# Token-major projections of two slots at a time with 512 moving columns, and one doubling of the memory keys

## The chip, the core and the metric

The kernel runs on one core of one Trainium2 chip. The metric is the device time of one launch in microseconds (us). TensorE (PE) multiplies and transposes, VectorE (DVE), ScalarE (ACT) and GpSimd (POOL) do the element-wise work, and the DMA transfers of this kernel are issued from the queue of SyncE (SP) and, for a few tables, from POOL's.

## What is computed

One layer of an encoder trunk for one batch of 2048 tokens of width 1024. All mixers read one normed input through one projection of 11 slots of 256 columns:

```python
h = rmsnorm(x, norm_g[l])
proj = h @ w_in[l]
a_u, a_v, a_g, b_q, b_k, b_v, b_g, c_in, c_g, d_q, d_g = jnp.split(proj, N_IN_SLOTS, axis=-1)
y_a = chunked_spatial_gating(a_u, a_v, ...) * jax.nn.silu(a_g)
y_b = neighbourhood_attention(b_q, b_k, b_v, ...) * jax.nn.silu(b_g)
y_c = fourier_mixing(c_in, fn_w[l]) * jax.nn.silu(c_g)
mem_n = rmsnorm(mem, mem_norm_g[l])
y_d = memory_attention(d_q, mem_n, w_mkv, ...) * jax.nn.silu(d_g)
x = x + jnp.concatenate([y_a, y_b, y_c, y_d], axis=-1) @ w_out[l]
```

The neighbourhood attention has 4 heads of 64 on a token grid of 32 rows by 64 columns, the memory attention 4 heads over 256 memory tokens; queries and keys of both are normed by head.

## The kernel before

Everything is float32. Each large product is made from a high and a low part of both operands (three matmuls: high by high, high by low, low by high). The tokens are worked in two halves `h` of 1024.

**The projection slots.** `slot` (L201) runs one slot of 256 columns for one half of the tokens into four PSUM banks `acc` (pool `ps_acc`, four banks in all). In the slots of `NATURAL` (L948: a_v, b_q, b_k, b_v, d_q) the tokens are the stationary side and the result has tokens on the partitions: 8 blocks of 128 tokens, two to a bank, 192 matmuls with 256 moving columns. The other slots have the weights on the stationary side and 512 tokens as moving columns, 96 matmuls a slot. One weight tile, 256 rows of `w_in` in 256 columns, serves 48 matmuls of a natural slot.

**The weights.** `get_w` (L187) loads a tile into `raw` (256 KB, SP queue), ACT casts the high part (L196) and POOL subtracts it for the low part (L198). The pool `wp` has six buffers "hilo", so three tiles of a high and a low part each can be there: one in use and two ahead, in every slot.

**What follows a slot.** The PSUM banks are read by ACT and DVE in turns (`evac_nat`, L307, into `nat`, five buffers). The queries and keys are normed (`head_norm`: POOL squares L323, DVE sums L325, POOL power through L108 and L109, DVE multiplies L328), transposed on PE, split, and written to DRAM. `do_bv` (L378) writes the values of the neighbourhood attention in parts of 256 columns (ACT L385, DVE L386). `do_a` (L583) norms a_v. `mem_kv` (L392) makes keys and values of the memory (matmuls into two `sc` banks, squares of the memory rows on ACT L420, then ACT L427 and L430 out of `sc`, head_norm), and `mem_k` (L438) doubles the columns of the keys with eight DVE copies of 128x128 (L447, two buffers `sq`), each before one transpose, in two groups of four.

**The order.** PE's order is fixed by hand. `drive` runs a generator of projection slots, then `out_proj`, and between its steps the tasks that were spawned with a delay: mixers, transposes, attention units. The delay counts in a planner's time, which adds up matmul columns. A task waits for names in `self.done`. The other engines' instructions are ordered by a scheduler with the priorities given by `hp`, and each engine runs its own row in that order. `main` (L978) has the order of slots; the neighbourhood attention is spawned at L1040 and starts when "fft", "b_q1" and "d_q1" are done. It opens its SBUF pool where the Fourier mixer's was, and loads `kk`, `kl`, `qq` (L784, L785), `vt` (L761) and `bt` (L771).

Of the kernel before, what the change touches and what calls it, by code (L numbers as in the profile page):

```python
# [20 lines left out]
GW = 256  # L21
HD = 64
# [25 lines left out]
class Kern:  # L48
# [151 lines left out]

    def slot(self, h, c0, natural, ps, kstep):  # L201
# [105 lines left out]
    def evac_nat(self, h, ps, bank):  # L307
        nc = self.nc
        q = self.nat.tile([128, 512], F32, name="nat")
        with self.hp(8000):  # L310
            for j in range(2):
                o, i = q[:, j * 256:(j + 1) * 256], ps[bank][:, j * 256:(j + 1) * 256]
                r = self.rstd[h][:, bank * 2 + j:bank * 2 + j + 1]
                if j:
# [16 lines left out]
    def transpose_pairs(self, q):  # L331
        ps = self.ps_mi.tile([128, 512], F32, name="mi")
        for pr in range(2):
            for j in range(2):
                self.tr(ps[:, pr * 256 + j * 128:pr * 256 + j * 128 + 128],
                        q[:, j * 256 + pr * 128:j * 256 + pr * 128 + 128])
        return ps.rearrange("p (a b) -> p a b", a=2)

    def do_bqk(self, h, ps, kind, key):
        nc = self.nc  # L340
        with self.hp(8000):
            qs = [self.head_norm(self.evac_nat(h, ps, b)) for b in range(4)]
        yield 14.0 if key == "d_q0" else 6.5
        for b in range(4):
            with self.hp(8000):
                t = self.transpose_pairs(qs[b])
                hl = [self.st.tile([128, 2, 256], F32R, name="st") for _ in range(2)]
                hi, lo = hl
                for a in range(2):
                    ta, ha, la = t[:, a], hi[:, a], lo[:, a]  # L350
                    if kind == "q":
                        ta = ta.rearrange("p (r b c) -> p r b c", b=4, c=16)
                        ha, la = (v.rearrange("p (b r c) -> p r b c", b=4, c=16) for v in (ha, la))
                    elif kind == "k":
                        ta = ta.rearrange("p (r c) -> p r c", r=4)
                        ha, la = (v.rearrange("p (c r) -> p r c", r=4) for v in (ha, la))
                    if kind == "k":
                        nc.scalar.activation(out=ha, in_=ta, func=AF.Copy, scale=self.gqk[:, 0:1])
                        nc.vector.scalar_tensor_tensor(out=la, in0=ta, scalar=self.gqk[:, 0:1], in1=ha.bitcast(F32),
                                                       op0=ALU.mult, op1=ALU.subtract)  # L360
                    elif kind == "q":
                        self.evac_split(ha, la, ta)
                if kind == "d":
                    self.evac_split(hi, lo, t)
                gg = h * 4 + b
                for i in range(2):
                    src = hl[i].bitcast(F32)
                    if kind == "q":
                        nc.sync.dma_start(
                            out=self.QB[:, i, gg // 2, :, :, gg % 2, :].rearrange("p a b x -> p (a b) x"),  # L370
                            in_=src.rearrange("p a b -> p (a b)").rearrange("p (y x) -> p y x", x=64))
                    else:
                        dst = self.KB[i] if kind == "k" else self.QD[i]
                        nc.sync.dma_start(out=dst[:, :, gg * 256:(gg + 1) * 256], in_=src)
# [782 lines left out]
```

## Time and profile before

| | us |
|---|---|
| median of 3 runs (885.18 to 885.97) | 885.59 |
| profiled execution | 883.6 |
| its span, first to last instruction | 881.8 |
| PE busy | 860.3 (98% of the span) |
| DVE busy | 496.3 (56%) |
| ACT busy | 380.2 (43%) |
| POOL busy | 323.6 (37%) |

The page gives for each engine the time in which it worked. A wait of an engine is put down to the instruction that released it. For PE the page and the list of waits matter most: a stretch in which PE has no idle time has a length that is the number of its matmuls times the time from one start to the next, which I call the pitch. The granted clock of TensorE was 0.992 of full speed on average.

### The profile page before, as it was taken

The page shows a single profiled execution, that of the slowest core. Times are in us where ns is not written, and L with a number is a line of the kernel's source. Part 1 is how long each engine was busy: PE and PEld are TensorE (multiplying, and loading weights), DVE is VectorE, ACT ScalarE, POOL GpSimd, SP SyncE. Part 2 cuts the span into 40 slices and gives each one's busy share as a digit, 9 for nine tenths or more (in the row PEclk, how much of TensorE's full clock was granted, in tenths as well). Part 3 has the DMA queues.
Part 4 walks back from the last instruction along what each step waited for, and adds up shares of the span by engine and source line. Part 5 has one row for each costly group of instructions (what it writes and reads, how often), then busy time and mean ns, then how long its engine had stood idle before and what let it go on. Part 6 is the DMA issues. An engine that isn't in the chain of part 4 may idle for free. (4 is left out here: it accounts for less than half of the span.)

```text
span 881.8 us, 15020 instructions
## 1 busy us (share of the span) xinstructions
PE 860.3 (98%) x5216; PEld 757.5 (86%) x5216; DVE 496.3 (56%) x1084; ACT 380.2 (43%) x881; POOL 323.6 (37%) x354
## 2 busy tenths in 40 slices
PE   7999899999999999999999999999979999999998
PEld 6999689999878889999998788888868888888886
DVE  4336753776122746753246766676877776863331
ACT  5664333545532532332313445565874444531110
POOL 1148411752142222754165323453564433321110
PEclk8999999999999999999999999999999999999999
DMA  7956232336933661449669687865789977645752
GB/s 234 356 190 214 95 128 77 102 108 177 287 108 102 211 198 37 129 128 234 192 197 317 198 272 221 270 204 171 220 237 297 322 234 227 200 134 174 225 184 81
DMA packets 142717, 169.59 MB, mean 192 GB/s; under 512 B 28704, under 2 KB 104368, under 8 KB 142640
## 3 DMA queue, kind: packets, MB, share of 16 engines
q1 hardware_dynamic: 140912, 162.33, 58.6%
q0 software_dynamic: 1728, 6.29, 2.5%
q8 instruction: 41, 0.67, 0.3%
q14 instruction: 36, 0.29, 0.1%
HBM read 124.53 MB, written 44.05 MB: 191 GB/s over the span
## 5 line engine op out<-in xcount | busy, mean ns | idle before, releaser
L131 PE MATMUL acc<-hilo 128*128 128x512 f32 (+1 forms) x3648 | 716.2, 344 | 8.3 <-DVE st L296 4.9
L131 PEld LDWEIGHTS acc<-hilo 128*128 128x128 f32 x3648 | 560.3, 190 | 70.7 <-DVE st L296 5.7
L198 POOL TENSOR_TENSOR hilo<-raw,hilo 128x512 fp32r<-128x512 f32 x84 | 113.1, 1346 | 287.9 <-ACT hilo L196 268.4
L196 ACT CAST hilo<-raw 128x512 fp32r<-128x512 f32 x84 | 51.9, 618 | 109.9 <-PE acc L131 90.8
L904 POOL TENSOR_TENSOR nat<-nat 128x256 f32<-128x256 f32 x39 | 30.9, 794 | 111.2 <-DMA nat<-O 73.9
L458 DVE TENSOR_TENSOR PT<-mi,PT 128x512 fp32r<-128x512 f32 (+2 forms) x96 | 61.1, 637 | 9.5 <-ACT PT L457 9.5
L457 ACT CAST PT<-mi 128x512 fp32r<-128x512 f32 (+2 forms) x96 | 52.2, 544 | 26.9 <-PE mi L135 26.4
L910 ACT CAST hilo<-nat 128x256 fp32r<-128x256 f32 x64 | 26.0, 406 | 75.4 <-PE acc L131 65.0
L839 ACT ACTIVATE P<-P,smx 128x288 f32<-128x288 f32 (+1 forms) x64 | 39.8, 622 | 40.9 <-DVE smx L837 40.7
L135 PE MATMUL mi<-ident,P 128*128 128x128 f32 (+1 forms) x352 | 54.3, 273 | 2.4 <-DVE P L842 1.7
L135 PEld LDWEIGHTS mi<-ident,P 128*128 128x128 f32 (+1 forms) x352 | 42.4, 135 | 15.5 <-DVE PT L458 2.3
L296 DVE TENSOR_TENSOR st<-acc,rbc 128x512 f32<-128x512 f32 x32 | 21.9, 685 | 37.9 <-PE acc L131 36.1
L109 POOL TENSOR_TENSOR hss<-hss,mhalf 128x8 f32<-128x8 f32 x25 | 41.9, 1680 | 0.9
L879 POOL TENSOR_TENSOR ob<-tmp 64x128 f32<-64x128 f32 x64 | 29.5, 479 | 33.3 <-DVE tmp L875 30.3
L911 DVE TENSOR_TENSOR hilo<-nat,hilo 128x256 fp32r<-128x256 f32 x64 | 33.1, 526 | 14.7 <-ACT hilo L910 14.5
L530 ACT ACTIVATE P<-sc,smx 128x256 f32<-128x256 f32 x64 | 29.7, 469 | 22.6 <-DVE smx L526 22.5
L122 DVE SCALAR_TENSOR_TENSOR hilo<-raw,gcol,hilo 128x512 fp32r<-128x512 f32 x32 | 24.9, 796 | 22.5 <-ACT hilo L121 22.0
L842 DVE TENSOR_SCALAR P<-P,smx 128x288 f32<-128x288 f32 (+1 forms) x64 | 36.1, 564 | 1.8
L837 DVE CUSTOM_DVE_ANT_0 P<-sc,bt 128x288 f32<-128x288 f32 (+1 forms) x64 | 35.6, 556 | 2.1 <-DMA bt<-in_bias 0.9
L131 PEld LDWEIGHTS mi<-PT,vt 96*128 96x128 f32 (+1 forms) x160 | 28.3, 193 | 6.9 <-issue 0.7
L875 DVE TENSOR_TENSOR tmp<-mi,tmp 64x512 f32<-64x512 f32 x32 | 22.0, 687 | 20.4 <-ACT tmp L874 20.2
L131 PE MATMUL mi<-PT,vt 96*128 96x256 f32 (+3 forms) x160 | 32.5, 334 | 0.3 <-DVE PT L458 0.2
(152 smaller groups left out, 971.1 us busy)
## 6 DMA issues: line engine op xcount, KB each, us to landing
raw<-in_w_in SPq DMA_DIRECT2D x88, 256.0 KB, 3.5
raw<-in_xT SPq DMA_DIRECT2D x32, 256.0 KB, 3.5
nat<-in_x SPq DMA_DIRECT2D x32, 256.0 KB, 5.1
G<-st SPq DMA_DIRECT2D x32, 256.0 KB, 2.5
nat<-G SPq DMA_DIRECT2D x64, 128.0 KB, 2.4
st<-in_x SPq DMA_DIRECT2D x32, 256.0 KB, 4.7
out_y<-st SPq DMA_DIRECT2D x32, 256.0 KB, 3.8
tab<-in_dft_s POOLq DMA_DIRECT2D x12, 512.0 KB, 4.8
```

What stands on the lines that cost most here:

```text
L109: nc.gpsimd.tensor_tensor(out=out, in0=out, in1=self.mhalf[:, :n], op=ALU.pow)
L131: self.nc.tensor.matmul(out=out, lhsT=lhsT, rhs=rhs, start=start, stop=stop, **k)
L135: self.nc.tensor.transpose(out=out, in_=in_, identity=self.ident)
L196: nc.scalar.copy(out=w[0], in_=raw)
L198: eng.tensor_tensor(out=w[1], in0=raw, in1=w[0].bitcast(F32), op=ALU.subtract)
L457: self.nc.scalar.copy(out=hi, in_=src)
L458: (eng or self.nc.vector).tensor_tensor(out=lo, in0=src, in1=hi.bitcast(F32), op=ALU.subtract)
L837: nc.vector.tensor_tensor_reduce(out=P[:, :n], in0=sc[:, :n], in1=bt[:, :n], op0=ALU.add, op1=ALU.min, scale=-1.0, scalar=3e38, accum_out= ...
L839: nc.scalar.activation(out=P[:, :n], in_=P[:, :n], func=AF.Exp, bias=sm[:, 1:2], scale=-1.0, accum_out=sm[:, 2:3])
L842: nc.vector.tensor_scalar(out=P[:, :n], in0=P[:, :n], scalar1=sm[:, 3:4], scalar2=None, op0=ALU.mult)
L904: mul.tensor_tensor(out=g, in0=o, in1=g, op=ALU.mult)
L911: nc.vector.tensor_tensor(out=y[:, 1], in0=g, in1=y[:, 0].bitcast(F32), op=ALU.subtract)
```

## The change

`pair` runs two slots together: b_q with b_k (`pair_qk`) and a_v with b_v (`pair_vv`). For each half `u` of the 1024 tokens (512 tokens) it takes four blocks of 128 tokens, one PSUM bank each, with 512 moving columns: 256 of the one slot and 256 of the other. In each half of each pair there are 96 matmuls. With two pairs, two token halves `h` and two halves `u` that is 768 matmuls of 512 columns in the place of 1536 of 256. d_q stays as it was.

`get_w2` loads 128 rows of `w_in` in 2 x 256 columns, as one tile of the old size. Each step of `pair` (24 matmuls) uses two tiles, A and B: for each of the four token blocks three matmuls on A and then three on B. Each half `u` loads all eight tiles again: 64 tiles in the place of 32, so 32 more loads of 256 KB, 32 more casts on ACT and 32 more subtractions on POOL. The pool `wp` keeps its six buffers.

What follows a slot now runs per half `u`. In the pair of a_v and b_v the evacuation of a_v (`do_a`) is spawned and that of b_v (`do_bv`) runs at once, so it stands ahead; both read every bank of the half. In `mem_kv` one DVE operation doubles all 512 columns into a tile "PT", and the delay of `mem_k` is 8.0 for 7.0. The constants of a_v's mixer are a task with a wait of 12.0. The values pair comes first for the first 1024 tokens. The attention waits for "fft" and "b_qk1" alone.

```diff
+    def get_w2(self, k, ia, ib):
+        nc = self.nc
+        with self.hp(8000):
+            raw = self.raw.tile([128, 2, 256], F32, name="raw")
+            src = self.ins["w_in"][k * 128:(k + 1) * 128, :].rearrange("p (s c) -> p s c", c=GW)
+            nc.sync.dma_start(out=raw, in_=src[:, ia:ib + 1:ib - ia, :])
+            w = [self.wp.tile([128, 2, 256], F32R, name="hilo") for _ in range(2)]
+            nc.scalar.copy(out=w[0], in_=raw)
+            nc.gpsimd.tensor_tensor(out=w[1], in0=raw, in1=w[0].bitcast(F32), op=ALU.subtract)
+        return [v.rearrange("p a b -> p (a b)") for v in w]
+
+    def pair(self, h, ca, cb, fn):
+        for u in range(2):
+            ps = [self.ps_acc.tile([128, 512], F32, name="acc") for _ in range(4)]
+            for k0 in range(0, 8, 2):
+                ops = [(self.get_x(h, k)[u], self.get_w2(k, ca // GW, cb // GW)) for k in (k0, k0 + 1)]
+                for t in range(4):
+                    sl = slice(t * 128, (t + 1) * 128)
+                    for k, ((xh, xl), (wh, wl)) in enumerate(ops, k0):
+                        self.mm(ps[t], xh[:, sl], wh, k == 0, False)
+                        self.mm(ps[t], xh[:, sl], wl, False, False)
+                        self.mm(ps[t], xl[:, sl], wh, False, k == 7)
+                    yield
+            fn(h, u, ps)
...
-    def do_bv(self, h, ps):
-        nc = self.nc
+    def do_bv(self, h, u, ps):
+        nc = self.nc
         with self.hp(8000):
-            for t in range(8):
+            for j in range(4):
+                t = u * 4 + j
                 v = self.nat.tile([128, 4, 2, 64], F32R, name="nat")
-                p = ps[t // 2][:, (t % 2) * 256:(t % 2) * 256 + 256].rearrange("p (g d) -> p g d", d=HD)
+                p = ps[j][:, 256:512].rearrange("p (g d) -> p g d", d=HD)
...
-        self.spawn(self.mem_k(q), 7.0)
+        twice = self.att.tile([128, 512, 2], F32, name="PT", bufs=2)
+        nc.vector.tensor_copy(out=twice, in_=q.unsqueeze(2).broadcast_to([128, 512, 2]))
+        self.spawn(self.mem_k(twice), 8.0)
...
-                    twice = self.sqp.tile([128, HD, 2], F32, name="sq")
-                    nc.vector.tensor_copy(out=twice, in_=q[:, c0:c0 + HD].unsqueeze(2).broadcast_to([128, HD, 2]))
-                    self.tr(ps[:, hh, j * 128:j * 128 + 128], twice.rearrange("p d o -> p (d o)"))
+                    self.tr(ps[:, hh, j * 128:j * 128 + 128],
+                            twice[:, c0:c0 + HD].rearrange("p d o -> p (d o)"))
...
-    def do_a(self, h, ps):
+    def do_a(self, h, u, ps):
...
-            for b in range(4):
-                v = self.evac_nat(h, ps, b)
+            for b in range(2):
+                v = self.evac_nat(h, [(ps[2 * b + j][:, 0:256], u * 4 + 2 * b + j) for j in range(2)])
...
+    def pair_qk(self, h):
+        yield from self.pair(h, B_Q, B_K, lambda h, u, ps: self.spawn(self.do_bqk(h, u, ps), 0, -1))
+
+    def pair_vv(self, h):
+        def fn(h, u, ps):
+            self.spawn(self.do_a(h, u, ps), 0, -1)
+            self.do_bv(h, u, ps)
+        yield from self.pair(h, A_V, B_V, fn)
...
-        yield from self.proj(0, "a_v")
+        self.spawn(self.constants_a(), 0, -2)
+        yield from self.pair_vv(0)
         self.spawn(self.when(("mem", "d_q0"), lambda: self.pipeline(self.d_items(0, range(4)), DLY["d0"])), 0, 1)
-        self.constants_a()
         yield from self.proj(0, "a_u")
-        for q in ("b_k", "b_q", "b_v", "a_g"):
-            yield from self.proj(0, q)
+        yield from self.pair_qk(0)
+        yield from self.proj(0, "a_g")
...
-        yield from self.proj(1, "b_k")
-        yield from self.proj(1, "b_q")
-        yield from self.proj(1, "b_v")
+        yield from self.pair_qk(1)
+        yield from self.pair_vv(1)
...
-        self.spawn(self.when(("fft", "b_q1", "d_q1"), attn), 0, 1)
-        for q in ("d_q", "a_v", "a_u", "a_g", "d_g", "b_g", "c_g"):
+        self.spawn(self.when(("fft", "b_qk1"), attn), 0, 1)
+        for q in ("d_q", "a_u", "a_g", "d_g", "b_g", "c_g"):
             yield from self.proj(1, q)
```

**The first place: PE, where the Fourier mixer ends and the attention begins.** `sc<-tab,ab` are the mixer's last matmuls, `acc<-hilo` those of the running slot (d_q of the second half of the tokens), `kk`, `kl` and `qq` the attention's keys and queries. Before:

```order
L131 MATMUL sc<-tab,ab 128x512 x12
L131 MATMUL acc<-hilo 128x256 x132
L135 MATMUL mi<-ident,nat 128x128 x4
L131 MATMUL acc<-hilo 128x256 x30
L135 MATMUL mi<-ident,nat 128x128 x4
L131 MATMUL acc<-hilo 128x256 x30
L135 MATMUL mi<-ident,nat 128x128 x4
L131 MATMUL acc<-hilo 128x256 x30
L135 MATMUL mi<-ident,nat 128x128 x4
L131 MATMUL acc<-hilo 128x256 x30
L131 MATMUL sc<-kk,qq 128x288
L131 MATMUL sc<-kl,qq 128x288
L131 MATMUL acc<-hilo 128x256 x6
L131 MATMUL sc<-kk,qq 128x384
```

And now:

```order
L131 MATMUL acc<-hilo 128x512 x12
L131 MATMUL acc<-hilo 128x256 x6
L131 MATMUL sc<-tab,ab 128x512 x12
L131 MATMUL sc<-kk,qq 128x288
L131 MATMUL sc<-kl,qq 128x288
L131 MATMUL acc<-hilo 128x256 x6
L131 MATMUL sc<-kk,qq 128x384
L131 MATMUL sc<-kl,qq 128x384
L131 MATMUL mi<-wsT,nat 64x128 x8
L131 MATMUL sc<-kk,qq 128x384
L131 MATMUL sc<-kl,qq 128x384
L131 MATMUL acc<-hilo 128x256 x6
```

The attention's first matmuls stood behind 252 matmuls of 256 columns; now they stand directly behind the mixer's last twelve.

**The second place: ACT, at the end of the first half `u` of the first values pair.** L196 and, in the changed kernel, L208 are casts of weight tiles; L317 (now L343) takes 256 columns of a bank into `nat`; L423 (now) is the b_v evacuation; L427, L430, L432 (now L465, L468, L470) take the memory's keys and values out of `sc`; L458 (now) squares memory rows. Before, where a_v's slot ends:

```order
L427 ACTIVATE nat_1121<-sc_780,rm_1117 128x256
L430 ACTIVATE sq_1129<-sc_780,rm_1117 128x256
L432 CAST vm_1122<-sq_1124 128x4x64
L317 ACTIVATE nat_1164<-acc_718,rstd0_563 128x256
L432 CAST vm_1122<-sq_1129 128x4x64
L317 ACTIVATE nat_1176<-acc_719,rstd0_563 128x256
L317 ACTIVATE nat_1188<-acc_720,rstd0_563 128x256
L196 CAST hilo_1423<-raw_1421 128x512
L317 ACTIVATE nat_1200<-acc_721,rstd0_563 128x256
L450 ACTIVATE sq_1283<-mi_1270,gqk_157 128x512
L457 CAST km0_1268<-sq_1283 128x512
L450 ACTIVATE sq_1321<-mi_1308,gqk_157 128x512
```

And now, where the first half of the values pair ends:

```order
L423 ACTIVATE nat_1084<-acc_721,rstd0_563 128x4x64
L343 ACTIVATE nat_1110<-acc_718,rstd0_563 128x256
L343 ACTIVATE nat_1122<-acc_720,rstd0_563 128x256
L458 ACTIVATE nat_1135,mss_1134<-nat_1135 128x512
L458 ACTIVATE nat_1138,mss_1134<-nat_1138 128x512
L208 CAST hilo_1213<-raw_1211 128x512
L458 ACTIVATE nat_1141,mss_1134<-nat_1141 128x512
L208 CAST hilo_1278<-raw_1276 128x512
L458 ACTIVATE nat_1144,mss_1134<-nat_1144 128x512
L465 ACTIVATE nat_1151<-sc_775,rm_1147 128x256
L468 ACTIVATE sq_1154<-sc_775,rm_1147 128x256
L465 ACTIVATE nat_1151<-sc_776,rm_1147 128x256
```

The bank that the next half fills first (`acc_718`) is read for a_v behind the b_v reads of all four banks, and the squares of the memory rows, which stood far ahead, now stand behind these reads and between casts of later weight tiles.

**The third place: POOL, behind a slot or a half of queries and keys.** L198 and, in the changed kernel, L209 are the subtractions for the low parts of weights; L323 (now L349), L108 and L109 belong to `head_norm`. Before, behind b_k of the first half of the tokens:

```order
L198 TENSOR_TENSOR hilo_2147<-raw_2144,hilo_2146 128x512
L323 TENSOR_TENSOR sq_1937<-nat_1934 128x512
L109 TENSOR_TENSOR hss_1919<-hss_1919,mhalf_153 128x8
L108 TENSOR_SCALAR hss_1929<-hss_1929 128x8
L108 TENSOR_SCALAR hss_1939<-hss_1939 128x8
L109 TENSOR_TENSOR hss_1929<-hss_1929,mhalf_153 128x8
L109 TENSOR_TENSOR hss_1939<-hss_1939,mhalf_153 128x8
L198 TENSOR_TENSOR hilo_2260<-raw_2257,hilo_2259 128x512
```

And now, behind the first half `u` of the queries and keys pair of the same tokens:

```order
L108 TENSOR_SCALAR hss_2014<-hss_2014 128x8
L349 TENSOR_TENSOR sq_2030<-nat_2028 128x512
L109 TENSOR_TENSOR hss_2014<-hss_2014,mhalf_153 128x8
L209 TENSOR_TENSOR hilo_2001<-raw_1998,hilo_2000 128x512
L108 TENSOR_SCALAR hss_2023<-hss_2023 128x8
L209 TENSOR_TENSOR hilo_2100<-raw_2097,hilo_2099 128x512
L349 TENSOR_TENSOR sq_2039<-nat_2037 128x512
L108 TENSOR_SCALAR hss_2032<-hss_2032 128x8
L109 TENSOR_TENSOR hss_2023<-hss_2023,mhalf_153 128x8
L109 TENSOR_TENSOR hss_2032<-hss_2032,mhalf_153 128x8
L108 TENSOR_SCALAR hss_2041<-hss_2041 128x8
L209 TENSOR_TENSOR hilo_2106<-raw_2103,hilo_2105 128x512
```

Between two subtractions there now stand up to five operations of `head_norm`, and each subtraction is for a tile that the next step needs.

## Rows read from the trace of the kernel before

**Rows 1.** Part 1 of the page: busy time, share of the span, instructions.

```profile
PE 860.3 (98%) x5216; PEld 757.5 (86%) x5216; DVE 496.3 (56%) x1084; ACT 380.2 (43%) x881; POOL 323.6 (37%) x354
```

**Rows 2.** What PE waited for: engine and line, us in total, times, longest.

```profile
PE acc L131 <- DVE st L296: 4.9, 2, 4.3
PE mi L135 <- DVE sq L447: 2.9, 2, 2.2
...
PE mi L135 <- DVE nat L328: 0.8, 1, 0.8
```

**Rows 3.** PE in order of time: start, length, line, tiles, count, idle time.

```profile
444.71 16.00 PE L131 MATMUL acc<-hilo 128*128 128x256 f32 x132
...
476.68 0.30 PE L131 MATMUL sc<-kk,qq 128*128 128x288 f32 x1
```

**Rows 4.** Stretches with L131 alone: length, PE and PEld busy, clock, DMA share, GB/s.

```profile
444.71:460.55 15.84, 15.84 (x133) 15.79 (x131) 1.00 0.66 218
245.87:316.08 70.21, 70.21 (x309) 57.96 (x309) 1.00 0.49 158
```

**Rows 5.** PE in order of time, slot matmuls beside attention.

```profile
122.42 1.55 PE L131 MATMUL acc<-hilo 128*128 128x512 f32 x6
123.81 0.60 PE L135 MATMUL mi<-ident,P 128*128 128x128 f32 x4
...
136.44 1.60 PE L131 MATMUL acc<-hilo 128*128 128x256 f32 x12
137.88 0.60 PE L135 MATMUL mi<-ident,P 128*128 128x128 f32 x4
```

**Rows 6.** PE in order of time, the transposes of the memory keys.

```profile
98.67 1.09 PE L131 MATMUL mi<-wsT,nat 128*64 128x128 f32 x16 [0.58 <-DVE nat L597]
99.70 0.44 PE L135 MATMUL mi<-ident,sq 128*128 128x128 f32 x2
102.29 0.47 PE L135 MATMUL mi<-ident,sq 128*128 128x128 f32 x2 [2.15 <-DVE sq L447]
```

**Rows 7.** ACT in order of time, same columns, a cast of a weight tile.

```profile
137.28 0.62 ACT L196 CAST hilo<-raw 128x512 fp32r<-128x512 f32 x1 [1.85 <-PE acc L131]
```

**Rows 8.** POOL in order of time, the subtraction behind that cast.

```profile
137.98 1.29 POOL L198 TENSOR_TENSOR hilo<-raw,hilo 128x512 fp32r<-128x512 f32 x1 [5.93 <-ACT hilo L196]
```

**Rows 9.** POOL, groups by line: count, busy us, mean ns, idle and releasers.

```profile
L198 POOL TENSOR_TENSOR hilo<-raw,hilo 128x512 fp32r<-128x512 f32 x84 | 113.1, 1346 | 287.9 <-ACT hilo L196 268.4 <-DVE tmp L875 12.7 <-DMA raw<-in_w_in 6.2
L109 POOL TENSOR_TENSOR hss<-hss,mhalf 128x8 f32<-128x8 f32 x25 | 41.9, 1680 | 0.9
...
L323 POOL TENSOR_TENSOR sq<-nat 128x512 f32<-128x512 f32 x25 | 26.0, 1045 | 9.0 <-DVE nat L315 6.8 <-DVE vm L433 1.8
```

**Rows 10.** ACT in order of time, memory keys read out of their bank.

```profile
88.25 0.47 ACT L427 ACTIVATE nat<-sc,rm 128x256 f32<-128x256 f32 x1 [0.92 <-PE sc L131]
```

**Rows 11.** SP queue in order of time: attention loads of keys and queries.

```profile
450.84 0.55 SPq L784 DMA_DIRECT2D kk<-KB  x1
...
452.27 0.59 SPq L785 DMA_DIRECT2D qq<-QB  x1
```

**Rows 12.** The records of the tile kk: its DMA from issue to landing.

```profile
DMA to landing us min/median/max: 5.2/5.2/5.2
```

**Rows 13.** Stretches of all engines: length, busy (count), PE clock, DMA share, GB/s.

```profile
450.84:461.30 10.46, 10.46 (x90) 10.46 (x89) 4.81 (x9) 2.51 (x6) 9.46 (x11) 1.00 0.95 296
657.00:664.00 7.00, 4.68 (x13) 3.91 (x14) 6.57 (x6) 4.74 (x13) 7.00 (x7) 0.52 0.96 297
```

**Rows 14.** PE in order of time, two longer waits.

```profile
481.60 0.50 PE L135 MATMUL mi<-ident,P 128*96 128x128 f32 x3 [1.66 <-DVE P L842]
...
659.32 1.65 PE L131 MATMUL acc<-hilo 128*128 128x512 f32 x3 [4.28 <-DVE st L296]
```

**Rows 15.** ACT, the squares of memory rows: count, busy us, mean ns, idle.

```profile
L420 ACT ACTIVATE nat<-nat 128x512 f32<-128x512 f32 x4 | 2.5, 636 | 4.7 <-DMA nat<-in_mem 4.7
```

**Rows 16.** POOL in order of time, behind the squares of the memory keys.

```profile
93.78 0.20 POOL L108 TENSOR_SCALAR hss<-hss 128x8 f32<-128x8 f32 x1 [2.08 <-DVE sa L592]
```

More of the change, by code (lines that the diff above doesn't have):

```diff
@@ L305, in evac_gate, with evac_nat @@
         self.evac_T(h, ps, fn)
-    def evac_nat(self, h, ps, bank):
+    def evac_nat(self, h, parts):
         nc = self.nc
         q = self.nat.tile([128, 512], F32, name="nat")
+        n = 512 // len(parts)
         with self.hp(8000):
[L311 to L314, printed above, removed]
+            for j, (i, t) in enumerate(parts):
+                o = q[:, j * n:(j + 1) * n]
+                r = self.rstd[h][:, t:t + 1]
+                if t % 2:
                     nc.vector.tensor_scalar(out=o, in0=i, scalar1=r, scalar2=None, op0=ALU.mult)
@@ L329, in head_norm, with transpose_pairs @@
         return q
[L331 removed]
+    def transpose_pairs(self, srcs):
         ps = self.ps_mi.tile([128, 512], F32, name="mi")
@@ L334, in transpose_pairs, with emit_T @@
             for j in range(2):
-                self.tr(ps[:, pr * 256 + j * 128:pr * 256 + j * 128 + 128],
-                        q[:, j * 256 + pr * 128:j * 256 + pr * 128 + 128])
+                self.tr(ps[:, pr * 256 + j * 128:pr * 256 + j * 128 + 128], srcs[j][:, pr * 128:pr * 128 + 128])
         return ps.rearrange("p (a b) -> p a b", a=2)
-    def do_bqk(self, h, ps, kind, key):
+    def emit_T(self, kind, gg, srcs):
         nc = self.nc
         with self.hp(8000):
-            qs = [self.head_norm(self.evac_nat(h, ps, b)) for b in range(4)]
-        yield 14.0 if key == "d_q0" else 6.5
-        for b in range(4):
[L345 to L374, printed above, removed]
-            yield 3.3
-        self.done.add(key)
@@ new lines, in emit_T @@
+            if kind == "d":
+                self.evac_split(hi, lo, t)
+            for i in range(2):
+                src = hl[i].bitcast(F32)
+                if kind == "q":
+                    nc.sync.dma_start(
+                        out=self.QB[:, i, gg // 2, :, :, gg % 2, :].rearrange("p a b x -> p (a b) x"),
+                        in_=src.rearrange("p a b -> p (a b)").rearrange("p (y x) -> p y x", x=64))
+                else:
+                    dst = self.KB[i] if kind == "k" else self.QD[i]
+                    nc.sync.dma_start(out=dst[:, :, gg * 256:(gg + 1) * 256], in_=src)
@@ new lines, in do_dq, with do_bqk @@
+    def do_dq(self, h, ps):
+        with self.hp(8000):
+            qs = [self.head_norm(self.evac_nat(h, [(ps[b][:, j * 256:(j + 1) * 256], 2 * b + j) for j in range(2)]))
+                  for b in range(4)]
+        yield 6.5 if h else 14.0
+        for b in range(4):
+            self.emit_T("d", h * 4 + b, [qs[b][:, 0:256], qs[b][:, 256:512]])
+            yield 3.3
+        self.done.add(f"d_q{h}")
+    def do_bqk(self, h, u, ps):
+        with self.hp(8000):
+            qs = [self.head_norm(self.evac_nat(h, [(ps[t], u * 4 + t)])) for t in range(4)]
+        yield 6.5
+        for b in range(2):
+            for i, kind in ((1, "k"), (0, "q")):
+                self.emit_T(kind, h * 4 + u * 2 + b, [qs[2 * b + j][:, i * 256:(i + 1) * 256] for j in range(2)])
+                yield 3.3
+        if u:
+            self.done.add(f"b_qk{h}")
@@ L600, in do_a @@
         yield 4.0
-        for b in range(4):
+        for b in range(2):
             with self.hp(8000):
@@ L946, in out_proj @@
                     nc.sync.dma_start(out=self.out[r0:r0 + 128, c * 512:(c + 1) * 512], in_=xt)
-    NATURAL = ("a_v", "b_q", "b_k", "b_v", "d_q")
+    NATURAL = ("d_q",)
     def proj(self, h, *which):
@@ L970, in after @@
     def after(self, h, which, ps):
-        key = which + str(h)
-        if which in ("b_q", "b_k", "d_q"):
-            self.spawn(self.do_bqk(h, ps, {"b_q": "q", "b_k": "k", "d_q": "d"}[which], key), 0, -1)
-        elif which == "b_v":
-            self.do_bv(h, ps)
-        elif which == "a_v":
-            self.spawn(self.do_a(h, ps), 0, -1)
+        if which == "d_q":
+            self.spawn(self.do_dq(h, ps), 0, -1)
         elif which == "a_u":
```

21 lines of the change are left out of this document (19 added, 2 removed).

## Prediction

> **What bounds the kernel now.** I read the busy shares first [rows 1]: PE works 98% of the span, no other engine above 56%. So a saving on another engine is worth nothing by itself, and whatever makes PE wait is paid in full. Next, the list of what PE waited for [rows 2]: its largest item is 4.9 us at the start of the output product, and all its waits together are small beside the span. PE is lined up without gaps, so the change is the sum of two things: how much less time its matmuls take, and which new waits they meet.
>
> Then I read stretches without any other PE work. The reader is to see the pitch: the 256-column matmuls start every 15.84 / 132 = 120.0 ns (the count of 132 is from the timeline [rows 3]), the 512-column ones every 70.21 / 309 = 227.2 ns [rows 4]. In the 256-column stretch the weight loads are as busy (15.79 us) as the stretch is long. That is what the change goes for.
>
> **The gain.** Two matmuls of 256 cost 240.0 ns, one of 512 costs 227.2; the difference of 12.8 ns times 768 is 9.8 us. The other bound is from stretches with attention work between: 12 of 256 take 1.44 us, 6 of 512 take 1.39 [rows 5], so 8.3 ns a pair, 6.4 us. I take 9.8, since most of the pairs' stretches hold little else. The Trainium skill, page "TensorE: Matmul & The Clock Gate", section "Wait — 56ns, not 53.3ns?", says that a warm matmul takes its columns at 2.4 GHz and about 2.5 ns more, whatever its size. By it two of 256 would cost 218.3 ns, one of 512 215.8, and the change would give 2.5 ns x 768 = 1.9 us (an estimate from that page). By it the sum below would end 7.9 us higher. The rows do not bear it out, at 240.0 and 227.2.
>
> The eight copies of the memory keys go, and with them the waits on them, 2.9 us [rows 2]: one buffer pair held back the copies. Two more waits lie in code that changes: 0.8 for a normed key tile [rows 2], 0.6 for the mixing of a_v [rows 6]. All together 4.3. Gains: 14.1 us.
>
> **Weight tiles that come too late.** In `slot` one tile serves 48 matmuls, and two wait behind it. In `pair` a step of 24 matmuls, 24 x 0.227 = 5.45 us, uses two of the three tiles. The next A tile takes the third place and is early. The next B tile takes the place of the old A, which is free only three matmuls before the step ends; its low part is wanted as the fifth matmul on from the next step's start. That is seven matmuls, 1.59 us. What has to happen in them: the cast starts 0.12 us after the release (the sixth of the matmuls from 136.44 ends at 136.44 + 6 x 0.12 = 137.16, the cast starts at 137.28 [rows 5, 7]), the subtraction 0.70 us later [rows 7, 8], and it takes 1.35 us on average [rows 9]: 2.17 us. So PE waits 0.58 us. Other PE work that stands between covers some of it. In the order of the changed kernel 14 B tiles have 1.59 us, two 1.77, one 1.95, six 2.07, one 2.11; the rest are covered or open a slot. 14 x 0.58 + 2 x 0.40 + 0.22 + 6 x 0.10 + 0.06 = 9.8 us. With the 1.29 us of the single subtraction [rows 8] it is 8.1; where ACT is in the middle of a read of 0.47 when a tile comes free, some tiles are later still, and with 0.1 us each it is 12. This alone takes the gain of the pitch. The 32 more casts and subtractions are hidden otherwise: ACT and POOL are free more than half of the time.
>
> **POOL's row behind queries and keys.** Three halves of those pairs are followed by another half of a pair (the fourth by a gate slot, which has two tiles ahead). There `head_norm` stands before the next subtractions. With E the end of the half: the third block's bank is whole at E - 1.36, its read on ACT takes 0.12 + 0.47 [rows 7, 10], its square 1.05 [rows 9] till E + 0.28, a power 1.68 till E + 1.96, and only then the B subtraction, till E + 3.31 where E + 1.59 was wanted: a wait of 1.7 in the place of 0.6. In the next step the A subtraction, a square and two powers (1.35 + 1.05 + 2 x 1.68) run till E + 9.1, and the B subtraction ends at E + 10.4; it is wanted at E + 1.7 + 5.45 + 1.59 = E + 8.8, a wait of 1.6 for 0.6. The excess is 1.1 + 1.0, three times: 6.4 us. It is nothing if POOL gets through ahead, and 10 if the small operations count fully.
>
> **The banks at the end of a values half.** ACT reads the b_v part of all four banks, the last behind the half's last matmul, and then the a_v part of the first bank, which the next matmul waits for. From the end: 0.12 for the wake, a cast of 0.62, two reads of 0.47 each [rows 7, 10]: 1.7 us. Three ends have no other work to cover it, so 5.1 us (4 to 6).
>
> **The attention's start.** Before, the Fourier mixer's last matmul gave way to the slot at 444.71, and the attention's first matmul came at 476.68 [rows 3]. Its keys and queries were asked for at 450.84 to 452.27 [rows 11], so they were there. The asking hangs on the mixer's own end (its last results go out ahead on the same SP queue), not on the slot, so it stays some 6 to 8 us behind the mixer. Now the first score stands right behind the mixer, and all PE work queued behind it waits as well. The load of `kk` lands 5.2 us after its issue [rows 12]; for `qq` that gives 457.5 at the least. If all that is asked for by then shares the engines, 10.46 us x 296 GB/s = 3.1 MB [rows 13] are through at 461.3. PE would wait 12.8 to 16.6 us; I take the middle, 14.7. The clock comes on top: behind the idle 4.28 us at 655 [rows 14] the granted clock was 0.52 of full speed over 7 us, the lower of its levels, 1.2 GHz, and 4.68 busy us did the work of 2.4 [rows 13]: 2.3 us lost. The waits of 1.66 and 2.15 us [rows 6, 14] show none of that. Together 17.0.
>
> **The memory keys at the start.** Before, their squares and sums were done early, and from the read out of `sc` at 88.25 [rows 10] to the first transposes at 99.70 [rows 6] 11.45 us passed, beside a full slot. Now the last square of the memory rows stands on ACT behind a cast that waits for the end T of the second half's first step: T + 0.12 + 0.62 + 0.64 [rows 7, 15]. Behind it comes a power on POOL, 1.68 by the nearest row [rows 9], so the read starts at about T + 3.1. The 11.45 held a wait of 2.08 on POOL [rows 16] that may go: transposes at T + 12.5. PE is there after 12 matmuls, 16 small ones (98.67 to 99.70 [rows 6]) and a late weight tile, 2.7 + 1.0 + 0.6: T + 4.3. PE waits 8.1 us. It is nothing if the squares get ahead, 10.2 with the whole chain, and 2.3 more if the clock falls as well.
>
> **The sum.** -14.1 + 9.8 + 6.4 + 5.1 + 17.0 + 8.1 = +32.3 us. 883.6 + 32.3 = 915.9 for the profiled execution; the median of before lies 2.0 above its own: 918.
>
> **Rivals.** (1) All new waits are hidden, since the other engines are half idle: only the gains, 885.6 - 14.1 = 871.5. It is decided at the first score: if `qq` is asked for before the mixer ends, the hand-over is free; and each B tile has to be there in 1.59 us. Rows 7 and 8 speak against it. 0.08. (2) Queues run ahead at POOL and at the memory keys, the rest holds: 885.6 + 32.3 - 6.4 - 8.1 = 903.4. For it: POOL has 63% idle. Against it: each engine keeps its row's order. 0.26. (3) The hand-over to the attention is covered by something that I do not see, the rest holds: 918 - 17 = 901. 0.06. (4) The change does not give its gain, since the 120 ns are an effect of that stretch: from the rows, up to 9.8 more, 928. That is where the page's rule of 2.5 ns leads too. 0.06. (5) Gains and costs meet within 0.2% (what a measurement of this kernel can tell from no change): 0.02. Forecast: 0.52.
>
> **The numbers.** Faster holds (1) and a little of the others, 0.09; same 0.02; slower 0.89. The forecast's own range is 903 to 933. The range of 8 in 10 goes down to 892, where rival 2 has its small ends (weights 8.1, banks 4, hand-over 12.8 without the clock: 885.6 - 14.1 + 24.9 = 896.4) with a little room, and up to 932.
>
> **What would show it.** Right: pair stretches of 512 columns at 227 ns with gaps of some 0.6 us every 5.45 us, released by POOL's subtraction; gaps of 1.7 us released by ACT's read of a_v three times; one gap of 13 to 17 us at the first score, released by a DMA, and a lower granted clock behind it; a gap of about 8 us before the transposes of the memory keys. Wrong: the hand-over without a gap, or B tiles that are early, which would mean that the buffers come free sooner than I read.

## The result

| | before | changed |
|---|---|---|
| median, us | 885.78 (885.18 to 890.30, 4 runs) | 932.18 (926.52 to 935.62, 4 runs) |
| profiled execution, us | 883.6 | 926.5 |
| its span, us | 881.8 | 924.7 |
| PE busy, us | 860.3 (98%) | 862.9 (93%) |
| POOL busy, us | 323.6 (37%) | 365.7 (40%) |

The changed kernel takes 1.0506 times as long (95% interval 1.0439 to 1.0573). Its profiled execution is the shortest of its four; where I account for it below, the sum is 926.5 - 883.6 = 42.9 us. Differences of a few us between two versions say little where each has four runs: those of the changed kernel alone spread over 9.1 us.

First the page of the changed kernel, its part 1, against [rows 1]:

```profile
PE 862.9 (93%) x4448; PEld 716.4 (77%) x4448; DVE 499.2 (54%) x1069; ACT 396.5 (43%) x905; POOL 365.7 (40%) x386
```

PE issues 768 instructions fewer, as it should, and yet its busy time does not fall. Then what PE waited for (engine and line, us in total, times, longest), against [rows 2]:

```profile
PE sc L131 <- DMA qq<-QB: 15.7, 1, 15.7
PE acc L131 <- POOL hilo L209: 14.6, 18, 2.8
PE mi L135 <- DVE PT L475: 8.2, 1, 8.2
...
PE mi L135 <- DVE nat L354: 1.6, 1, 1.6
```

The three largest are new, and each is one of the predicted places: the queries of the attention, the subtractions of the pairs' weights (L209), and the memory keys (L475). Together 38.5 us. No row is a load of weights, so the 32 more loads hold PE up nowhere that the profile shows; the casts of the pairs' tiles (L208) found ACT idle for 46.8 us, 38.8 of them for a buffer that PE was still using.

PE in order of time shows each of them (start, length, line, tiles, count, idle time before):

```profile
82.64 2.47 PE L131 MATMUL acc<-hilo 128*128 128x512 f32 x10
85.55 0.73 PE L131 MATMUL acc<-hilo 128*128 128x512 f32 x2 [0.44 <-POOL hilo L209]
...
103.53 1.09 PE L131 MATMUL mi<-wsT,nat 128*64 128x128 f32 x16
112.87 1.09 PE L135 MATMUL mi<-ident,PT 128*128 128x128 f32 x4 [8.24 <-DVE PT L475]
...
364.77 2.89 PE L131 MATMUL acc<-hilo 128*128 128x512 f32 x12
367.50 0.61 PE L131 MATMUL mi<-G,PT 128*128 128x128 f32 x4
367.86 2.54 PE L131 MATMUL acc<-hilo 128*128 128x512 f32 x10
372.55 3.40 PE L131 MATMUL acc<-hilo 128*128 128x512 f32 x8 [2.15 <-POOL hilo L209]
...
382.82 0.74 PE L131 MATMUL acc<-hilo 128*128 128x512 f32 x2 [1.77 <-POOL hilo L209]
...
477.54 2.92 PE L131 MATMUL sc<-tab,ab 128*128 128x512 f32 x12
496.20 0.58 PE L131 MATMUL sc<-kk,qq 128*128 128x288 f32 x1 [15.74 <-DMA qq<-QB]
```

How to read two of these lines. At 82.64 ten matmuls start; at 0.228 us each they give way at 84.92, but the next starts at 85.55: 0.63 us are lost, while the list shows 0.44. The end of a matmul is modelled and covers a part of each wait. Counted like this, from start to start, the 18 waits on L209 cost 17.6 us: twelve short ones of 0.43 to 0.60 (5.8) and six long ones of 1.2 to 3.0 (11.8). Second line: twelve matmuls of 512 columns in a pair take 367.50 - 364.77 = 2.73 us, 227.5 ns each. The pitch is as forecast. With every matmul at the usual pitch of its kind, PE's work is 836.3 us, before it was 844.6: the gain is there, 8.3 us.

The clock falls behind the long waits (length, busy time of PE, PEld, DVE, ACT, POOL, granted clock, DMA share, GB/s), against the second line of [rows 13]:

```profile
112.00:120.00 8.00, 6.79 (x25) 5.38 (x25) 2.34 (x3) 3.54 (x6) 1.43 (x2) 0.69 0.00 0
370.00:380.00 10.00, 7.85 (x33) 6.21 (x32) 5.02 (x7) 0.99 (x2) 9.51 (x10) 0.83 0.17 52
496.00:504.00 8.00, 7.80 (x62) 6.84 (x63) 4.55 (x15) 2.48 (x7) 0.00 (x0) 0.79 1.03 375
```

At the two levels of 1.2 and 2.4 GHz the busy time of these stretches held 2.1, 1.3 and 1.6 us of loss (busy time times what is missing to 1.00).

**The subtractions.** POOL in order of time, at the end of the first half `u` of queries and keys of the second half of the tokens:

```profile
368.63 1.04 POOL L349 TENSOR_TENSOR sq<-nat 128x512 f32<-128x512 f32 x1
369.63 1.64 POOL L109 TENSOR_TENSOR hss<-hss,mhalf 128x8 f32<-128x8 f32 x1
371.24 1.26 POOL L209 TENSOR_TENSOR hilo<-raw,hilo 128x512 fp32r<-128x512 f32 x1
...
373.18 1.27 POOL L209 TENSOR_TENSOR hilo<-raw,hilo 128x512 fp32r<-128x512 f32 x1
374.41 1.04 POOL L349 TENSOR_TENSOR sq<-nat 128x512 f32<-128x512 f32 x1
375.53 0.20 POOL L108 TENSOR_SCALAR hss<-hss 128x8 f32<-128x8 f32 x1
375.81 3.23 POOL L109 TENSOR_TENSOR hss<-hss,mhalf 128x8 f32<-128x8 f32 x2
379.13 0.70 POOL L108 TENSOR_SCALAR hss<-hss 128x8 f32<-128x8 f32 x1
379.91 1.64 POOL L109 TENSOR_TENSOR hss<-hss,mhalf 128x8 f32<-128x8 f32 x1
381.51 2.96 POOL L209 TENSOR_TENSOR hilo<-raw,hilo 128x512 fp32r<-128x512 f32 x2
```

The subtraction at 371.24 ends at 372.50, and PE goes on at 372.55. The next one, at 373.18, is in time; the one after it, for which PE then waits till 382.82, stands behind a square and three powers. POOL has no gap here: 9.51 of the 10 us from 370.

**The memory keys.** ACT in order of time, the third square of the memory rows, a cast of a weight tile, the last square, and the read out of PSUM:

```profile
101.30 0.63 ACT L458 ACTIVATE nat<-nat 128x512 f32<-128x512 f32 x1 [1.53 <-DMA nat<-in_mem]
...
101.93 0.60 ACT L208 CAST hilo<-raw 128x512 fp32r<-128x512 f32 x1
102.44 0.63 ACT L458 ACTIVATE nat<-nat 128x512 f32<-128x512 f32 x1
...
104.99 0.47 ACT L465 ACTIVATE nat<-sc,rm 128x256 f32<-128x256 f32 x1 [1.84 <-POOL rm L109]
```

Before, that read was at 88.25 with 11.45 us to the transposes [rows 10, 6]; now it is at 104.99 with 7.88. What held the squares up was their own loads: ACT stood idle for 1.53 us till the third row had landed, and the cast behind it, at 101.93, found ACT busy and waited for nothing else (the step whose end releases it was over at 99.56, where other work begins on PE). The third row was asked for only at 97.40, when the first square had ended (96.65 + 0.63) and given back its buffer `nat`, of which there are five; the loads of the first two waited for stores of b_v values out of the same buffers.

**The attention's start.** SP's queue in order of time:

```profile
486.18 0.55 SPq L824 DMA_DIRECT2D kk<-KB  x1
...
487.75 0.58 SPq L825 DMA_DIRECT2D qq<-QB  x1
```

The mixer's last matmul gives way at 477.54 + 12 x 0.228 = 480.28; the keys are asked for 5.9 us later, the queries 7.5, and the first score starts 8.4 us behind that.

### The profile page after: what moved, and what is told of

Same layout as the page of the kernel before. It is cut to its first block, busy times and chain, and to the rows that moved or that the text cites. A ratio compares the mean times of both kernels' runs of the same rounds, so it can differ in the third digit from the quotient of the medians.

```text
span 924.7 us, 13637 instructions
## 1 busy us (share of the span) xinstructions
PE 862.9 (93%) x4448; PEld 716.4 (77%) x4448; DVE 499.2 (54%) x1069; ACT 396.5 (43%) x905; POOL 365.7 (40%) x386
## 4 chain that ended last, share of the span: by engine, by line
PE 68%; DMA 6%; POOL 5%; DVE 4%; issue 2%; ACT 2%; SPq 1%; POOLq 0%; DVEq 0%; ACTq 0%
PE acc L131 54%; PE mi L131 5%; PE sc L131 5%; PE mi L135 5%; POOL hilo L209 2%; DMA qq<-QB 2%; DMA nat<-O 1%; DMA nat<-in_x 1%; POOL hss L109 1%; DMA bt<-in_bias 1%; DVE hilo L951 1%; POOL sq L349 1%; DVE PT L497 0%; ACT nat L269 0%; POOL hss L108 0%
## 5 line engine op out<-in xcount | busy, mean ns | idle before, releaser
L131 PE MATMUL acc<-hilo 128*128 128x512 f32 (+1 forms) x2880 | 716.4, 392 | 22.7 <-POOL hilo L209 14.6
L131 PEld LDWEIGHTS acc<-hilo 128*128 128x128 f32 x2880 | 513.3, 190 | 122.4 <-POOL hilo L209 24.4
L198 POOL TENSOR_TENSOR hilo<-raw,hilo 128x512 fp32r<-128x512 f32 x52 | 69.0, 1329 | 178.3 <-ACT hilo L196 170.8
L209 POOL TENSOR_TENSOR hilo<-raw,hilo 128x512 fp32r<-128x512 f32 x64 | 84.0, 1327 | 115.0 <-ACT hilo L208 101.0
L497 DVE TENSOR_TENSOR PT<-mi,PT 128x512 fp32r<-128x512 f32 (+2 forms) x96 | 61.2, 638 | 11.8 <-ACT PT L496 11.4
L208 ACT CAST hilo<-raw 128x512 fp32r<-128x512 f32 x64 | 39.7, 620 | 46.8 <-PE acc L131 38.8
L877 DVE CUSTOM_DVE_ANT_0 P<-sc,bt 128x288 f32<-128x288 f32 (+1 forms) x64 | 35.6, 556 | 20.1 <-DMA bt<-in_bias 16.2
L196 ACT CAST hilo<-raw 128x512 fp32r<-128x512 f32 x52 | 32.2, 618 | 32.9 <-PE acc L131 24.4
L109 POOL TENSOR_TENSOR hss<-hss,mhalf 128x8 f32<-128x8 f32 x25 | 41.4, 1661 | 0.8
L131 PE MATMUL sc<-kk,qq 128*128 128x288 f32 (+1 forms) x64 | 22.7, 355 | 15.7 <-DMA qq<-QB 15.7
L882 DVE TENSOR_SCALAR P<-P,smx 128x288 f32<-128x288 f32 (+1 forms) x64 | 33.3, 521 | 2.0
```

Source lines behind the costliest of these rows:

```text
L109: nc.gpsimd.tensor_tensor(out=out, in0=out, in1=self.mhalf[:, :n], op=ALU.pow)
L131: self.nc.tensor.matmul(out=out, lhsT=lhsT, rhs=rhs, start=start, stop=stop, **k)
L198: eng.tensor_tensor(out=w[1], in0=raw, in1=w[0].bitcast(F32), op=ALU.subtract)
L208: nc.scalar.copy(out=w[0], in_=raw)
L209: nc.gpsimd.tensor_tensor(out=w[1], in0=raw, in1=w[0].bitcast(F32), op=ALU.subtract)
L497: (eng or self.nc.vector).tensor_tensor(out=lo, in0=src, in1=hi.bitcast(F32), op=ALU.subtract)
```

## Experiments

The theory: three waits, each with its own cause, make up the loss, and the matmul gain stands beside them. The rivals: the waits stand in for each other, so that one undone brings the next; and, for the subtractions, that it is not the buffers but POOL.

| kernel | us (median) | ratio to before, 95% |
|---|---|---|
| changed | 932.2 | 1.0506 [1.0439, 1.0573] |
| e_loop | 930.9 | 1.0529 [1.0468, 1.0590] |
| e_hyb | 930.3 | 1.0502 [1.0447, 1.0557] |
| e_mem | 925.0 | 1.0456 [1.0415, 1.0496] |
| e_attn | 921.6 | 1.0434 [1.0378, 1.0489] |
| e_dve | 913.8 | 1.0318 [1.0284, 1.0352] |
| e_delay | 913.4 | 1.0326 [1.0283, 1.0370] |
| e_three | 911.6 | 1.0304 [1.0243, 1.0364] |
| e_six | 896.4 | 1.0105 [1.0064, 1.0145] |
| e_four | 895.4 | 1.0117 [1.0088, 1.0145] |
| e_five | 888.8 | 1.0047 [1.0024, 1.0071] |
| e_seven | 885.2 | 0.9998 [0.9983, 1.0014] |
| before | 884 to 885.8 | 1 |
| e_keys | 881.9 | 0.9954 [0.9932, 0.9975] |

**Buffers free earlier (e_loop).**

```diff
-                for t in range(4):
-                    for k, ((xh, xl), (wh, wl)) in enumerate(ops, k0):
+                for k, ((xh, xl), (wh, wl)) in enumerate(ops, k0):
+                    for t in range(4):
...
```

> The changed kernel with one exchange of loops in the pair: all four token blocks on tile A, then all four on tile B, so that A's buffers come free 12 matmuls before the step ends instead of 3. Theory (the B tiles are late because their buffers come free late, and POOL's row adds to it six times): the waits on the subtraction, 17.6 us counted from start to start in the profile of the changed kernel, go, and some 1.4 us of half clock behind one of them: 932 - 19 = 913 us, 907 by the profiled execution. Rival (POOL is too slow for 32 more subtractions, or their order is what counts, whatever the buffers do): 928 or more, with waits on the subtraction of over 10 us left.

930.9 us: nothing gained, and the time is the rival's. But its waits are not where either put them. What PE waited for:

```profile
PE sc L131 <- DMA qq<-QB: 14.2, 1, 14.2
PE mi L135 <- DVE nat L355: 12.1, 7, 3.1
PE mi L135 <- DVE PT L476: 10.4, 1, 10.4
```

No wait on a subtraction of the pairs (L209) is left in the list; in their place stand seven waits for normed queries and keys (L355, the last step of `head_norm`), and the memory keys wait longer. The tiles come in time, and the norming, on the same POOL, does not. Two causes were open: the banks come whole up to 2 us later in this order of loops (the first one nine matmuls later), or POOL is full.

**Buffers free earlier, banks whole as early as in the changed kernel (e_hyb).** The last step of each half keeps its order:

```diff
+                turns = [(t, j) for t in range(4) for j in range(2)]
+                if k0 < 6:
+                    turns = [(t, j) for j in range(2) for t in range(4)]
...
```

> The changed kernel with the loops exchanged (four blocks on A, then four on B) in the first three steps of a half, and as they were in the last step, so that the banks of a half come whole as early as in the changed kernel. Theory (POOL is full while queries and keys run): the waits on the subtraction fall below 6 us, but waits on the normed queries and keys of 6 us or more come in their place, as with the loops exchanged everywhere (12.1 us): 922 to 930 us. Rival (those new waits came from the banks that were whole 2 us later): they stay below 3 us, 915 us.

930.3 us. The waits:

```profile
PE mi L135 <- DVE nat L358: 8.2, 6, 1.9
...
PE acc L131 <- POOL hilo L209: 1.6, 1, 1.6
```

The subtraction falls from 14.6 to 1.6, and 8.2 us for the normed rows come for it; other waits grow by up to 1.8 us (the memory keys from 8.2 to 9.9, L769 from 0.4 to 2.2). So the later banks were only a part (12.1 against 8.2). That POOL's row is what stays shows in e_four, below: it has these loops, among other edits, with the subtractions off POOL, and its wait for the normed rows is 1.3 us, once.

**The subtractions on DVE (e_dve).**

```diff
-            nc.gpsimd.tensor_tensor(out=w[1], in0=raw, in1=w[0].bitcast(F32), op=ALU.subtract)
+            nc.vector.tensor_tensor(out=w[1], in0=raw, in1=w[0].bitcast(F32), op=ALU.subtract)
```

> The changed kernel with the subtractions of the pairs' 64 weight tiles on DVE in the place of POOL, nothing else. Theory (POOL is full while queries and keys run: a half of 21.8 us brings 8 subtractions of 1.33 and 4 times 1.05 + 1.66 + 0.3 of norming, 22.7 us; without the subtractions it has 12): the six long waits (11.8 us together) go, and the short ones of about 0.5 become 0.1 or less, since DVE takes about 0.7 us; the norming is early too: 932 - 16 = 916 us. Rival (the delay only moves, DVE is late for the transposes and the memory attention): 925 or more, with over 10 us of new waits on DVE.

913.8 us, 18.4 less. The first two rows of the waits:

```profile
PE sc L131 <- DMA qq<-QB: 15.8, 1, 15.8
PE mi L135 <- DVE PT L475: 9.1, 1, 9.1
```

Of the waits on the subtraction 0.9 us are left, in three, and none on the normed rows has come for them (1.2 us on L354, where the changed kernel has 1.6); the loops and the buffers are those of the changed kernel. The 64 subtractions take 0.70 us each on DVE:

```profile
L209 DVE TENSOR_TENSOR hilo<-raw,hilo 128x512 fp32r<-128x512 f32 x64 | 44.2, 698 | 35.3 <-ACT hilo L208 30.0 <-PE acc L131 4.9 <-DMA KB<-st 0.3
```

0.12 + 0.70 + 0.70 = 1.52 us fits into the 1.59 of a late tile. The length of POOL's work was the cause, the one behind both the short waits and the long ones.

**The attention's start (e_attn, e_delay).** Once by the old condition, once by a wait behind the mixer:

```diff
-        self.spawn(self.when(("fft", "b_qk1"), attn), 0, 1)
+        self.spawn(self.when(("fft", "b_qk1", "d_q1"), attn), 0, 1)
```

> The changed kernel, with the attention waiting for d_q of the second half of the tokens again. Theory (the first score stands behind the mixer before its queries are there): the wait of 15.9 us goes, and about 1.5 us of half clock: 932 - 17 = 915 us. Rival (the attention that starts a slot earlier pays at the end, so the later start costs most of it again; or the wait moves to the biases or to the output product): 925 or more, with a new wait of over 8 us on PE behind it.

```diff
+            yield 17.0
             yield from self.pipeline(items(), DLY["b"])
```

> The changed kernel, with a wait of 17.0 of the planner's time between the end of the mixer and the attention's first score; the loads may go out at once. 114 matmuls of 256 columns and 16 small ones come between, 14.7 us. Theory (the first score stands 15.9 us ahead of its queries, and the place of the attention in the slots beyond that costs nothing): the wait falls to 2 us or less: 932 - 14 - 2 (half clock) = 916 us, below the 921.6 of the version where the attention waits for the whole slot of d_q. Rival (a later start of the attention costs at the end what it saves at the start): 920 to 925.

921.6 and 913.4 us: 10.6 and 18.8 less than the changed kernel. In e_delay 3.4 us of the wait are left:

```profile
PE sc L131 <- DMA qq<-QB: 3.4, 1, 3.4
```

Both expectations were met in part: the wait goes in e_attn and falls to 3.4 in e_delay, and in e_attn the attention pays for starting a whole slot later. Its list has waits on DVE that the changed kernel's has not in this size, most of them in the attention (behind 650 us):

```profile
PE mi L135 <- DVE PT L497: 5.5, 5, 1.8
PE mi L131 <- DVE od L506: 4.1, 3, 1.9
```

My reading is that with one slot less to lie beside it the attention meets DVE more often. The intervals of the two versions do not meet, so the early start was worth something, only not as early as the mixer's last matmul.

**The memory rows (e_mem).** The four squares and their sum stand ahead of the memory matmuls:

```diff
+        ss = self.c([128, 2, 2], "mss")
+        for t in range(2):
+            for u in range(2):
...
         ps = [self.ps_sc.tile([128, 512], F32, name="sc") for _ in range(2)]
```

> The changed kernel, with the squares of the memory rows ahead of the memory matmuls in the program, nothing else. Theory (the squares stand behind a cast that waits for a step's end, and the chain to the memory keys starts there): the wait of 8.5 us before the transposes of the memory keys goes down to 2 or less, and 1.4 us of half clock: 932 - 9 = 923 us. Rival (the chain behind the read out of PSUM is long enough by itself, whenever the squares are done): a wait of 5 us or more stays, 929 us.

925.0 us, 7.2 less; the wait on L475 goes from 8.2 to 1.9, and a wait of 2.0 for DVE comes at a broadcast before it. Those copies (L668) stand on DVE behind the low part of a memory row, for which DVE waited 2.64 us for ACT, and ACT had waited 3.05 us for the load of a square:

```profile
PE mi L135 <- DVE G L668: 2.0, 1, 2.0
PE mi L135 <- DVE PT L475: 1.9, 1, 1.9
```

So the place of the squares makes the wait. Whether they were late behind a cast or for their loads this edit cannot tell, since it moves both; the trace of the changed kernel, above, says the loads.

**Together (e_three, e_four, e_five).** e_three has the edits of e_loop, e_attn and e_mem.

> The three edits together. Theory (the three waits are independent and all that is left is PE's work): 932 - 19 - 17 - 9 = 887 us, near 885.6 of the kernel before, with PE's matmuls 8 us shorter than before and some 6 us of waits left on DVE in the memory attention of the first half. Rival (the waits stand in for each other: when one goes, another engine is late at the next place): 895 to 905.

911.6 us: over the rival's 895 to 905 too. With e_loop's norming and e_attn's late attention in it, two of its three edits bring their own waits. e_four has e_dve, e_hyb, e_attn, the squares between the memory matmuls, and mem_k's delay at 12.

> The changed kernel with the pairs' subtractions on DVE, the loops exchanged in the first three steps of a half, the attention behind d_q of the second half, the squares of the memory rows between the memory matmuls, and a delay of 12 for the memory keys. Theory (each wait of the change has its own cause, and with POOL relieved none comes in their place): PE's matmuls are 8 us shorter than before and the waits about as many: 880 us, between 876 and 888. Rival (DVE becomes the next one that PE waits for): 895 to 910.

895.4 us: the rival again. Its largest waits are for DVE, in the larger part in the attention (behind 630 us):

```profile
PE mi L135 <- DVE PT L502: 5.9, 4, 2.5
PE mi L131 <- DVE PT L502: 4.3, 4, 2.4
PE mi L131 <- DVE od L511: 4.1, 4, 1.9
```

e_five has e_dve, e_delay (the wait of 17.0, without the condition), the squares between the memory matmuls, and the delay of 12, with the loops of the changed kernel.

> The changed kernel with the subtractions on DVE, the wait of 17.0 before the first score, the squares of the memory rows between the memory matmuls, and a delay of 12 for the memory keys. Theory (three causes, each with its own cure, and the attention about where the changed kernel has it): 932 - 18 - 16 - 9 = 889, between 884 and 892, so about as fast as before. Rival (with the attention later, DVE holds PE up as in the version with four edits): 893 to 900.

888.8 us. The single effects of e_dve (18.4), e_delay (18.8) and e_mem (7.2) add up to 44.4 us; 932.2 - 44.4 = 887.8. So with cures that bring no wait of their own the three waits are nearly all of the loss, and none of them stands in for another: in e_five's list the queries are left with 2.7 us, L209 with 0.4, and the memory keys are gone. That the sum meets 888.8 within 1.0 us is luck in part, since each of the three differences has the spread of the changed kernel in it.

**Two trials to gain more (e_six, e_seven).** e_six moves the transposes of queries and keys from 6.5 to 10.0 behind their half:

> The version before this one in the list, with the transposes of queries and keys 10.0 behind their half in the place of 6.5. Theory (some 5 us of waits in the second quarter are transposes that come before the normed rows, or that DVE cannot empty beside the memory attention): 3 us less than that version. Rival (the delay pushes the same work into the memory attention's way elsewhere): the same within 1 us or more.

896.4 us, 7.6 more than e_five: the theory falls. Its largest wait is for the evacuation of slots, five times:

```profile
PE acc L131 <- DVE st L321: 8.7, 5, 2.6
```

e_seven is e_five with later places for the first score (21.0), the memory keys (14) and the broadcast (18), and the sum of the squares behind the matmuls:

> The version with four cures (888.8 us), with 21.0 in the place of 17.0 before the first score, 14 in the place of 12 for the memory keys, and the broadcast of the norms at 18 in the place of 15. Theory (its waits of 2.9 us for the queries and of 2.6 us before that broadcast are places of PE work set too early): 888.8 - 5 = 884, between 882 and 887. Rival (they stand in for waits that show up elsewhere): 887 to 891.

885.2 us, the same as before (ratio 0.9998). So the change, with everything cured that I found, comes out even. The one copy of the memory keys is in it, and that alone gives 3.0 us (e_keys, below), in an interval that does not meet this one: the pairs by themselves, cured, still cost about as much.

**The other half of the change alone (e_keys).** The kernel before with the one copy and the delay of 8.0:

> The kernel before with the memory keys doubled by one operation and the delay of 8.0, and no pairs. Theory (the two waits of 2.9 us on the copies go and nothing comes for them): 885.6 - 2.9 = 882.7, within 0.5 us. Rival (the keys' chain is as late with one operation): 885 to 886.

881.9 us, ratio 0.9954: clear of no change, and the only version clearly below the kernel before. The two waits of [rows 2] on L447 are gone from the list of waits, and nothing has come for them at the keys.

## Why the prediction came out

The forecast was 918 with a range of 892 to 932, and slower at 0.89; measured was 932.2, at the upper edge (the forecast's own range was 903 to 933), 14 above the forecast. The way and the three large places were right; by its steps:

- **The matmuls** (-9.8): 8.3 by the pitch in the changed kernel. Right. The rival that the pitch would not hold falls.
- **The memory key copies** (-2.9): right by e_keys, 3.0 between the medians of one sitting (884.8 and 881.9). Of the two other waits the 0.6 for the mixing of a_v is gone, too, the 0.8 is not: it is 1.6 now (L354).
- **Late weight tiles and POOL's row** (9.8 + 6.4 = 16.2): 17.6 by the starts, 18.4 by e_dve. The sum was right, its split not: the short waits are fewer and cheaper (12 of 0.48), the long ones dearer (11.8 with the short one in them, against 9.9). My cause was right in kind but told too little: I took the buffers and POOL's row as two causes. e_loop and e_hyb show that earlier buffers alone give nothing, since POOL then has the norming late.
- **Banks at the end of a values half** (5.1): 0.7, the step that failed. I took it that the next half's first block takes the first block's bank. It did not wait for that read: ACT read the a_v part late, as I had it, but PE had already gone on. ACT's reads, DVE's read of the a_v part of the second block, and PE:

```profile
93.97 0.47 ACT L423 ACTIVATE nat<-acc,rstd 128x256 fp32r<-128x256 f32 x1
94.34 0.83 ACT L343 ACTIVATE nat<-acc,rstd 128x256 f32<-128x256 f32 x2
...
91.80 0.47 DVE L341 TENSOR_SCALAR nat<-acc,rstd 128x256 f32<-128x256 f32 x1
...
92.07 2.43 PE L131 MATMUL acc<-hilo 128*128 128x512 f32 x10
94.81 4.83 PE L131 MATMUL acc<-hilo 128*128 128x512 f32 x20 [0.31 <-POOL hilo L209]
```

PE's ten matmuls from 92.07 are six of the old half and four of the new, which began at 92.07 + 6 x 0.227 = 93.43. A bank that had been read in full was free by then: DVE reads the a_v part of the second block, at 91.80, without standing in ACT's row. That the new half took this bank I infer; no row names banks. The order named the tiles by numbers, and I took the number for the bank. The 0.7 us are two waits for such a read on DVE (L341), where a values half gives way to another slot. The term was 4.4 too high and hid as much of what the sum lacked; that the result still fell into the range is luck to that extent.
- **The attention's start** (14.7, clock 2.3): 15.9 between the starts and 1.6 of clock: 17.5 against 17.0. The queries landed 8.4 us after they were asked for, near the upper bound (461.3 - 452.27 = 9.0).
- **The memory keys** (8.1): 8.5, and 2.1 of clock that I had only in the range. The place was right, the cause in part: I had the last square behind a cast that waits for the step's end T, and it was the squares' loads, late for want of buffers, that held the row up. With T at 99.5 the read out of `sc` started at T + 5.5 where I had T + 3.1, and the chain behind it took 7.9 us where I had 9.4. PE was there at T + 4.9, not T + 4.3. That the three nearly cancel is luck.
- **Not in the sum**: 5.7 us at 230 to 249, where the transposes of queries and keys meet the memory attention on DVE, and 1.3 us of half clock behind the wait of 2.15 us at 370.

In sum, counting every start that comes over 0.15 us later than the pitch (waits, and matmuls of 512 columns at half clock), 22.4 us were lost before and 69.4 are now; 47.0 more, less 8.3, and 4.2 in smaller pieces (slower clock and others): 42.9. The rest to the median, 3.5 us (46.4 - 42.9), is a difference between executions. The longer executions of the changed kernel have a lower mean clock (0.972 at 935.6 us, 0.979 at 926.5), so one more fall of the clock may be all of it; they have no trace, and it stays open. Open is also why some 4 to 6 us of waits in the second quarter (at 230 to 249 in the changed kernel) stay in every version of the pairs; e_six was to move them and made it worse.

## What to carry to other kernels

When two streams of operands are joined into wider matmuls, the same number of weight bytes serves fewer tokens at a time: count the loads, the casts and the subtractions per microsecond of PE, not per kernel, and set them against the stretch in which the preparing engine has something else to do. POOL was idle 60% of the time in the changed kernel, and its work still cost 18 us. An engine that orders its work once for all pays with the work that stands behind; move the work to another engine before buying buffers. And a start that is made earlier must be made earlier for its loads as well: here a wait of 17.0 of the planner's time behind the mixer was better than both ends.

## What the hardware showed that I had not expected

A wait of 2.15 us of PE (at 370) was followed by half clock, 0.83 on average over 370 to 380, though a wait of the same length before [rows 6] was not, nor the longest of these waits, 2.80 us up to 418.84 (granted clock 1.00 from 418.8 to 424). In e_delay the same wait and two others of the six were followed by it (0.57 over 375 to 379, 0.53 over 385.5 to 389.1, 0.57 over 423 to 427), in e_attn the same wait was not (1.00 over 376 to 380). So in these runs the length of a wait does not settle it. And a wait costs PE more than its list shows: 18 waits with 14.6 us of idle time cost 17.6 from start to start, since the modelled end of the last matmul covers 0.17 us of each.
